# A token-shift evacuation shared out between ScalarE and VectorE, and transposes moved one block back

## The chip, the cores and the metric

The kernel runs on one core of a Trainium2 chip. A core has TensorE (matrix products, PE in the profile; its weight loads are PEld), VectorE (DVE), ScalarE (ACT), GpSimd (POOL) and SyncE (SP), which here issues every DMA. Matrix products land in PSUM, eight banks that TensorE writes and that VectorE and ScalarE read; everything else lies in SBUF or in device memory. The metric is the device time of one execution in microseconds, lower is better; 0.5% of it is 7.8 us.

## The reference

One encoder layer is applied to two token sequences (512 and 256 tokens, width 1024): a hybrid mixer (eight heads of an RWKV-7 recurrence in both directions beside four heads of chunked gated linear attention, GLA), cross-attention to a memory of 256 tokens, and a feed-forward layer, each between RMS norms. What the change touches is the projection into the mixer and the centred shift behind it:

```python
def centred_shift(p, mu_prev, mu_next):
    prev = jnp.pad(p[:, :-1], ((0, 0), (1, 0), (0, 0)))
    nxt = jnp.pad(p[:, 1:], ((0, 0), (0, 1), (0, 0)))
    return p + mu_prev * (prev - p) + mu_next * (nxt - p)

def hybrid_mixer(h, p):
    proj = h @ p['w_in']
    rw = centred_shift(proj[..., :R_COLS], p['mu_prev'], p['mu_next']).astype(jnp.float32)
    gl = proj[..., R_COLS:].astype(jnp.float32)
    mixed = jnp.concatenate([rwkv7_group(rw, p), gla_group(gl, p)], axis=-1).astype(h.dtype)
    return mixed @ p['w_out']
```

The first 1952 columns of the projection (receptance, key, value of the RWKV heads and the small low-rank inputs) are shifted: each token's value is mixed with those of the token before and after it, with weights per column. The other columns (query, key, value, gate of the GLA heads) are not.

## The kernel before

**Tiling.** Activations are held with channels on the 128 partitions and tokens along the free axis. A projection block is 128 columns of `w_in` for all 768 tokens. Products are done in split precision: each operand is a rounded part and a remainder (hi, lo), and one product is three matmuls per 128 input channels (`mm3`, L243 to L250). `load_block` (L214) loads the weights in four pieces through SP, ScalarE rounds them (whi, L149) and VectorE takes the remainder (wlo, L150). `channels_product` (L252) then runs 24 matmuls for the 512-token sequence and 24 for the 256-token one, each sequence into one of the two PSUM buffers with tag "d" (`psd`, L72; the names pd, gvt and others share these two).

**Evacuation.** For a GLA block (`gla_dense`, L475) ScalarE copies the PSUM buffer into an SBUF tile (L482). For an RWKV block (`rkv_block`, L443) `shift_evac` (L318) applies the shift: ScalarE writes (1 − mu_prev − mu_next) times the product (L322), VectorE adds mu_prev times the product moved by one token (L324) and then mu_next times the product moved the other way (L327), both reading PSUM. There are 12 such RWKV blocks (four pairs of heads, `p`, times `i` = 0, 1, 2 for key, receptance, value). The four "small" blocks of the low-rank inputs use the same helper from `small_part` (L360).

**Where the result goes.** The output of a block is a tile `ot` of 128 x 768 with tag "gd". The pool `gdp` has two of these. A store writes it to device memory (`rkvd`, `gqk`, `ggd`). For values (`i` = 2 in `rkv_early`, L448; `g` = 3 in `gla_dense`) it is first turned with tokens on the partitions: `tokens_first` (L464) does six 128 x 128 transposes on TensorE into two "d" buffers (gvt, L470), VectorE copies them into another "gd" tile (L472), and stores follow, four of them for an RWKV pair (`vtd`, L457), one for a GLA block (`gvd`, L486). This second "gd" tile is taken through `gd2` (L459) from the pool in `more[0]`: `gdp` at first, and after GLA head 0 has been traced a pool `gdq` with two buffers of its own (L953).

**Order.** The program is written as a sequence; a scheduler at compile time keeps each engine's queue in the order of its own timeline, by priority (program order, with `tc.high_priority` raising what stands under it), and each engine then executes its queue in order. DMAs are issued in order by SP. The blocks of the stretch are traced in this order: pair 0 (key, receptance, value; L556 to L559), GLA blocks (0, 0), (1, 0), (3, 0), (2, 0) (L819; the first number 0 is the query, 1 the key, 3 the values, 2 the gate), preparation of pair 0 (`begin`), its triangular inverses (`invert`, 62 dependent VectorE operations, L749 to L754), `joined`; `gla_head(0)`; the blocks of pair 1 and (3, 1), (2, 1) (L954), `begin(1)`, `invert(1)`, `gla_head(1)`; (0, 1), (1, 1), (3, 2), (2, 2), `joined(1)`; pair 2 (L960), `gla_head(2)`, (3, 3), (2, 3), `begin(2)`, `invert(2)`, `gla_head(3)`; then the memory's planes (`memory`, L1120, in space that the GLA arena leaves), pair 3 (L1181), and the recurrence itself.

**What a GLA head reads.** `gla_head` (L835) loads its query, key, decay and values into an arena. The values come from `gvd` (L844); the first use of them is the product gds (L900), from which a recurrence of small VectorE operations (L911), the output products (go, L923 and L925), the gate and the store `mixd<-arena` (L949) follow. `begin` loads `wa<-lora` (L646), the decays of the pair, before VectorE's scans and products (L649 to L674).

Of the kernel before, what the change touches and what calls it, by code (L numbers as in the profile page):

```python
# [10 lines left out]
AF = mybir.ActivationFunctionType  # L11
ALU = mybir.AluOpType
# [4 lines left out]
P = 128  # L17
# [15 lines left out]
def kernel(ctx: ExitStack, tc: tile.TileContext, I, y_prompt, y_sample):  # L33
    nc = tc.nc
    act = nc.scalar
    dve = nc.vector
# [3 lines left out]
    def dma(out, in_):  # L40
        return nc.sync.dma_start(out=out, in_=in_)  # L41
# [30 lines left out]
    def psd(name):  # L72
        return ps.tile([P, 512], F32, tag="d", bufs=2, name=name)

    def psm(name):
        return ps.tile([P, 512], F32, tag="m", bufs=2, name=name)
# [15 lines left out]
    hT_hi = hp.tile([P, KD, T], F32R, tag="hh", name="hT_hi")  # L92
    hT_lo = hp.tile([P, KD, T], F32R, tag="hl", name="hT_lo")
# [41 lines left out]
    HS = (slice(0, 64), slice(64, 128))  # L135
# [107 lines left out]
    def mm3(out, pairs):  # L243

        n = 3 * len(pairs)
        i = 0
        for (ah, al), (bh, bl) in pairs:
            for a, b in ((ah, bh), (ah, bl), (al, bh)):
                pe.matmul(out=out, lhsT=a, rhs=b, start=(i == 0), stop=(i == n - 1))  # L249
                i += 1  # L250

    def channels_product(w, m, hi, lo, seqs=SEQS, wc0=0):  # L252

        res = []
        for c0, n in seqs:
            pd = psd("pd")
            mm3(pd[0:m, 0:n], [((wh[:, wc0:wc0 + m], wl[:, wc0:wc0 + m]),
                                (hi[:, k, c0:c0 + n], lo[:, k, c0:c0 + n])) for k, (wh, wl) in enumerate(w)])
            res.append((c0, n, pd))
        return res  # L260
# [4 lines left out]
    def w_cols(c0, n):  # L265
        return w_in[:, c0:c0 + n]
# [48 lines left out]
    def cvc(name, i=0):  # L315
        return cv[:, col[name] + i:col[name] + i + 1]

    def shift_evac(res, mu, dst, m=P):  # L318

        for c0, n, pd in res:  # L320
          with tc.high_priority():
            act.activation(out=dst(c0, n), in_=pd[0:m, 0:n], func=AF.Copy, scale=mu0[0:m, mu:mu + 1])  # L322
            o = dst(c0 + 1, n - 1)
            dve.scalar_tensor_tensor(out=o, in0=pd[0:m, 0:n - 1], scalar=cvc("mu_prev", mu)[0:m, :],  # L324
                                     in1=o, op0=ALU.mult, op1=ALU.add)
            o = dst(c0, n - 1)
            dve.scalar_tensor_tensor(out=o, in0=pd[0:m, 1:n], scalar=cvc("mu_next", mu)[0:m, :],  # L327
                                     in1=o, op0=ALU.mult, op1=ALU.add)

    with tc.high_priority(offset=9000):  # L330
        g_row = lp.tile([1, D], F32, tag="mnxn", bufs=2, name="g_row")
# [19 lines left out]
    for c in (0, 512):  # L351
        t = psm("g_ps")
# [7 lines left out]
    def small_part(i, part):  # L360
# [6 lines left out]
        if part != 1:  # L367
# [7 lines left out]
                      in1=cv[:, col["mu_next"]:col["mu_next"] + 16], op=ALU.add)  # L375
# [14 lines left out]
    for v in ("w0_f", "w0_b", "a0_f", "a0_b", "k_k", "k_a", "lnx_w", "lnx_b"):  # L390
# [11 lines left out]
                      op0=ALU.mult, op1=ALU.add)  # L402
# [10 lines left out]
    gvd = dp.tile([T, 512], F32, name="gvd")  # L413
# [13 lines left out]
    vtd = [dp.tile([2, 64, 6, 128], F32, name=f"vtd{p}") for p in range(4)]  # L427
# [15 lines left out]
    def rkv_block(p, i, dst):  # L443
        c0, mu = ((512, 4), (0, 0), (1024, 8))[i]
        w = load_block([(w_cols(c0 + p * P, P), 0)], P)
        shift_evac(channels_product(w, P, hT_hi, hT_lo), mu + p, dst)

    def rkv_early(p, i):  # L448

        ot = gdp.tile([P, T], F32, tag="gd", bufs=2, name="gd")  # L450
        rkv_block(p, i, lambda c, n: ot[:, c:c + n])
        dma(rkvd[p, i], ot)
        if i == 2:
            vt = tokens_first(ot)
            for h, hs in enumerate(HS):
                for par, ps_ in enumerate(HS):
                    dma(vtd[p][h][:, :, par * 64:par * 64 + 64], vt[ps_, :, hs])  # L457

    def gd2(name):  # L459
        return more[0].tile([P, T], F32, tag="gd", bufs=2, name=name)  # L460

    more = [gdp]

    def tokens_first(ot):  # L464

        vt = gd2("gd")
        for c, n in SEQS:
            pt = psd("gvt")
            for j in range(0, n, P):
                pe.transpose(out=pt[:, j:j + P], in_=ot[:, c + j:c + j + P], identity=ident)  # L470
            with tc.high_priority():
                dve.tensor_copy(out=vt[:, c:c + n], in_=pt[:, 0:n])  # L472
        return vt.rearrange("p (j e) -> p j e", e=P)

    def gla_dense(g, i):  # L475

        c0 = (1952, 2208, 2992, 2464)[g] + i * P
        w = load_block([(w_cols(c0, P), 0)], P)
        ot = gdp.tile([P, T], F32, tag="gd", bufs=2, name="gd")
        for c, n, pd in channels_product(w, P, hT_hi, hT_lo):  # L480
            with tc.high_priority():
                act.activation(out=ot[:, c:c + n], in_=pd[:, 0:n], func=AF.Copy)  # L482
        if g < 3:
            dma((gqk[i % 2], gqk[2 + i % 2], ggd[i])[g], ot)
            return
        dma(gvd.rearrange("(j p) e -> p j e", p=P)[:, :, i * P:(i + 1) * P], tokens_first(ot))  # L486

    if True:
        def stacked(name, groups, shape, put):
# [106 lines left out]
        for i in range(4):  # L596
# [3 lines left out]
            for k0 in range(0, KD, 4):  # L600
# [3 lines left out]
                ot = lp.tile([P, 4, P], F32, tag="mt", bufs=4, name="mt")  # L604
# [11 lines left out]
    for d in range(2):  # L616
        t = mp.tile([P, NCH, 64], F32, tag=f"tt{d}", name=f"tt{d}")
# [195 lines left out]

    def blocks(bs):
        for g, i in bs:
            gla_dense(g, i) if g < 4 else rkv_early(g - 3, i)

    sts = []
    blocks([(0, 0), (1, 0), (3, 0), (2, 0)])  # L819
# [163 lines left out]
    def lay_places():  # L983
        plh, pll = (hp.tile([P, KD * T], F32, tag=n, name="pl_" + n) for n in ("hh", "hl"))
        for t, gs in ((plh, (0, 4)), (pll, (1, 5))):
            for i, g in enumerate(gs):
                whole_place(g, t[:, 2560 * i:2560 * i + 2560])
        place(3, plh[:, 5120:5632], pll[:, 5120:5888], mq1.tile([P, 512], F32, tag="pl3", name="pl3"), plh[:, 5632:6144],
              pll[:, 5888:6144])
        whole_place(2, mq1.tile([P, 2560], F32, tag="pl2", name="pl2"))  # L990
# [188 lines left out]
    mq2 = mq2_cm.__enter__()  # L1179
    mem = memory()  # L1180
    blocks([(6, i) for i in range(3)])  # L1181
    lay_places()
    yas += [gdp.tile([P, T], F32, tag="gd", bufs=2, name=f"ya{i}") for i in range(2)]
    prods(0, (0, 4, 1, 5))
# [20 lines left out]
    for _ in range(BKBUFS):  # L1205
        t = mp.tile([P, 2, T], F32R, tag="bk", bufs=BKBUFS, name="mix_bk")
# [19 lines left out]
    for n in ("snf", "sqf"):  # L1226
        t = mp.tile([P, 2, 512], F32R, tag=n, name="w_" + n)
# [3 lines left out]
    t = mq1.tile([P, 5, 512], F32R, tag="pl2", name="w_pl2")  # L1231
# [82 lines left out]
    with tc.tile_pool(name="op1", bufs=1, reuse_waits="tile") as op1:  # L1314
# [8 lines left out]
        hT_hi, hT_lo = out_projection(op1, wt, mix, x_rows, rows, g_post, x1d, g_pre)  # L1323
# [9 lines left out]
    with tc.tile_pool(name="ao", bufs=1, reuse_waits="tile") as ao:  # L1333
# [18 lines left out]
        for h in range(4):  # L1352
# [16 lines left out]
            for s_, (c0, n) in enumerate(SEQS):  # L1369
# [25 lines left out]
                for e in range(2):  # L1395
# [3 lines left out]
                                     for m in range(2)])  # L1399
                    act.activation(out=oh[:, 2 * h + e, c0:c0 + n], in_=pm[:, 0:n], func=AF.Copy)  # L1400
                    dve.tensor_tensor(out=ol[:, 2 * h + e, c0:c0 + n], in0=pm[:, 0:n], in1=oh[:, 2 * h + e, c0:c0 + n],
                                      op=ALU.subtract)
# [6 lines left out]
        with tc.tile_pool(name="op2", bufs=1, reuse_waits="tile") as op2:  # L1409
# [10 lines left out]
            for i in range(6):  # L1420
                ts_ = slice(i * P, (i + 1) * P)
                pd = (psd, psy)[i % 2]("po")
# [63 lines left out]
    with tc.tile_pool(name="f1", bufs=1, reuse_waits="tile") as f1, tc.tile_pool(name="fw", bufs=1, reuse_waits="tile") as fw:  # L1486
# [98 lines left out]
        h = {"11": blk[0][0], "21": blk[1][0], "22": blk[1][1], "t1": blk[0][1]}  # L1585
# [32 lines left out]
        for at, (f, n) in enumerate(jobs):  # L1618
# [5 lines left out]
            for ct in range(2):  # L1624
# [4 lines left out]
                pd = st["z" if n in (0, 2, 4) else "x", ct][:, 0:384]  # L1629
# [43 lines left out]
        with tc.tile_pool(name="us", bufs=1, side="right", reuse_waits="tile") as us:  # L1673
# [46 lines left out]
            for at, (c, n, s_) in enumerate(jobs):  # L1720
# [3 lines left out]
                for t in range(3):  # L1724
# [4 lines left out]
                    pd = banks["z" if n in (0, 2, 4) else "x", t]  # L1729
# [3 lines left out]
                    if s_ % 2:  # L1733
                        i, half, new = TO[n]
                        i += t
                        o = acc[i][:, CS[half]]
# [34 lines left out]
```

## Time and profile before

| | |
|---|---|
| median of 3 runs | 1554.85 us (1549.77 to 1558.52) |
| the profiled execution | 1548.75 us |
| its span | 1546.6 us |
| mean granted TensorE clock in it | 0.93 |
| instructions | 27578 |
| TensorE matmul, weight load, VectorE, ScalarE, GpSimd busy | 91%, 77%, 70%, 46%, 14% |

The profile shows one execution. A group of instructions is written as its line, engine, operation and the tiles out<-in; "mean ns" is the duration of one of the group. A wait names the instruction that waited and what released it. The chain of work that ended last is followed back from the last instruction of the execution: each piece is what released the next. In the windows, each pair of columns is an engine's busy time and its instructions in that stretch; the last three columns are the granted TensorE clock (1 is full), the share of the DMA engines and their GB/s. All times of single instructions count from the start of the span.

### The profile page before, as it was taken

What the parts mean: (1) busy time and instruction counts of PE and PEld (TensorE: products, weight loads), DVE (VectorE), ACT (ScalarE), POOL (GpSimd) and SP (SyncE); (2) the same over time, 40 slices, a digit from 0 to 9 for tenths busy, and PEclk for the clock granted to TensorE, in tenths of its full rate; (3) what the DMA queues carried; (4) which work ended last, traced back from release to release, by engine and by line L of the source; (5) the groups of instructions that cost most, each with busy time, mean ns of one, the idle gap of its engine ahead of it and who ended that gap; (6) DMA issues with size and microseconds to landing.
All of it is one profiled execution on the core that took longest, in us unless ns stands there. A gap on an engine that the chain in (4) does not pass through costs nothing.

```text
span 1546.6 us, 27578 instructions
## 1 busy us (share of the span) xinstructions
PE 1408.3 (91%) x10238; PEld 1183.6 (77%) x10238; DVE 1076.7 (70%) x1913; ACT 706.0 (46%) x1477; POOL 220.9 (14%) x304
## 2 busy tenths in 40 slices
PE   7998899897799987999699999978999999999996
PEld 6886778775676766777478887868999998787785
DVE  5555896698567994866665554279766667788886
ACT  5664345443423442344353454345554555454342
POOL 5301000000000000003211233320000002132132
PEclk9999899987779996799799999988999999999998
DMA  6687666584468667464452332244554547555334
GB/s 165 177 314 210 171 197 156 167 228 102 128 187 232 180 184 168 106 166 144 128 179 98 107 100 79 82 154 155 196 170 153 181 157 291 155 175 172 120 103 136
DMA packets 279562, 250.30 MB, mean 162 GB/s; under 512 B 89264, under 2 KB 227059, under 8 KB 279428
## 3 DMA queue, kind: packets, MB, share of 16 engines
q1 hardware_dynamic: 279428, 248.54, 53.8%
q8 instruction: 81, 1.33, 0.4%
q14 instruction: 53, 0.43, 0.1%
HBM read 164.11 MB, written 82.58 MB: 160 GB/s over the span
## 4 chain that ended last, share of the span: by engine, by line
PE 59%; DVE 13%; DMA 11%; issue 8%; SPq 3%; ACT 3%; POOL 2%; DVEq 0%; ACTq 0%; POOLq 0%
PE pd L249 19%; PE fx L1548 7%; PE gx L1548 6%; PE fz L1548 5%; PE gz L1548 5%; SPq L41 3%; PE po L249 3%; DMA wraw<-in_w_in_dram 1%; DVE ws L1488 1%; PE hsum L639 1%; DVE wl L1539 1%; DMA raw<-in_w_out_dram 1%; PE xo L249 1%; POOL rs L1264 1%; PE bktp L1028 1%
## 5 line engine op out<-in xcount | busy, mean ns | idle before, releaser
L249 PE MATMUL pd<-hT_hi,whi 128*128 128x256 f32 (+1 forms) x512 | 183.5, 358 | 9.1 <-DVE gd L327 4.1
L249 PE MATMUL pd<-hT_lo,whi 128*128 128x256 f32 (+1 forms) x512 | 180.2, 352 | 0.3 <-DVE hT_lo L208 0.3
L249 PE MATMUL pd<-hT_hi,wlo 128*128 128x256 f32 (+1 forms) x512 | 178.5, 350 | 0.0
L149 ACT ACTIVATE whi<-wraw 128x256 fp32r<-128x256 f32 x192 | 77.5, 415 | 97.2 <-PE pd L249 59.4
L249 PEld LDWEIGHTS pd<-hT_hi,whi 128*128 128x128 f32 x512 | 100.9, 197 | 24.0 <-DVE gd L327 4.0
L150 DVE TENSOR_TENSOR wlo<-wraw,whi 128x256 fp32r<-128x256 f32 x192 | 80.2, 437 | 48.2 <-ACT whi L149 46.6
L249 PEld LDWEIGHTS pd<-hT_lo,whi 128*128 128x128 f32 x512 | 101.0, 197 | 13.1 <-DVE hT_lo L208 0.5
L249 PEld LDWEIGHTS pd<-hT_hi,wlo 128*128 128x128 f32 x512 | 100.2, 196 | 13.2 <-issue 0.5
L150 DVE TENSOR_TENSOR ul<-ur,uh 128x768 fp32r<-128x768 f32 x56 | 75.3, 1351 | 30.2 <-ACT uh L149 17.7
L149 ACT ACTIVATE uh<-ur 128x768 fp32r<-128x768 f32 x56 | 47.2, 845 | 106.6 <-PE gz L1548 51.8
L1538 ACT ACTIVATE wh<-w 128x1024 fp32r<-128x1024 f32 x64 | 67.1, 1053 | 36.7 <-PE fz L1548 24.2
L1539 DVE TENSOR_TENSOR wl<-w,wh 128x1024 fp32r<-128x1024 f32 x56 | 68.2, 1217 | 15.3 <-ACT wh L1538 14.7
L1548 PE MATMUL gx<-wh,uh 128*128 128x512 f32 x192 | 74.9, 397 | 4.2 <-DVE acc L1741 4.2
L1548 PE MATMUL gx<-wl,uh 128*128 128x512 f32 x192 | 75.9, 395 | 0.0
L1548 PE MATMUL gx<-wh,ul 128*128 128x512 f32 x192 | 75.4, 395 | 0.0
L1539 POOL TENSOR_TENSOR wl<-w,wh 128x1024 fp32r<-128x1024 f32 x8 | 20.9, 2610 | 329.3 <-ACT wh L1538 329.3
L1548 PE MATMUL fz<-hh,wh 128*128 128x384 f32 x192 | 66.1, 344 | 1.7 <-ACT wh L1538 1.7
L1548 PE MATMUL fz<-hl,wh 128*128 128x384 f32 x192 | 65.9, 343 | 0.0
L1548 PE MATMUL fz<-hh,wl 128*128 128x384 f32 x192 | 65.2, 344 | 0.6 <-DVE wl L1539 0.6
L1538 ACT ACTIVATE wh<-ws 128x1024 fp32r<-128x1024 f32 x48 | 50.5, 1052 | 27.2 <-PE fx L1548 22.5
L1548 PE MATMUL gz<-wl,uh 128*128 128x512 f32 x144 | 56.9, 395 | 0.0
L249 PE MATMUL pd<-mem_hi,wlo 128*128 128x512 f32 x128 | 56.0, 439 | 0.9 <-DVE wlo L150 0.9
(537 smaller groups left out, 3980.4 us busy)
## 6 DMA issues: line engine op xcount, KB each, us to landing
w<-in_w_ff_dram SPq DMA_DIRECT2D x64, 512.0 KB
ur<-ud SPq DMA_DIRECT2D x56, 384.0 KB
wraw<-in_w_in_dram SPq DMA_DIRECT2D x108, 128.0 KB
ud<-u SPq DMA_DIRECT2D x32, 384.0 KB
ud<-us SPq DMA_DIRECT2D x24, 384.0 KB
wraw<-in_wkv_x_dram SPq DMA_DIRECT2D x64, 128.0 KB
lora<-lo_t SPq DMA_DIRECT2D x20, 384.0 KB
bkg<-bkd SPq DMA_DIRECT2D x24, 256.0 KB
```

The lines of the kernel that those rows point to most:

```text
L41: return nc.sync.dma_start(out=out, in_=in_)
L149: act.activation(out=hi, in_=src, func=AF.Copy)
L150: (lo_eng or pool).tensor_tensor(out=lo, in0=src, in1=hi, op=ALU.subtract)
L249: pe.matmul(out=out, lhsT=a, rhs=b, start=(i == 0), stop=(i == n - 1))
L639: pe.matmul(out=pt[:, 0:n], lhsT=ones_bd, rhs=src[:, c0:c0 + n], start=True, stop=True)
L1028: pe.transpose(out=pt[:, u, :], in_=fl(b_[HS[h], u]), identity=ident[HS[h], HS[h]])
L1264: pool.tensor_tensor(out=rs, in0=ms, in1=neg_half, op=ALU.pow)
L1488: dve.tensor_tensor(out=out, in0=a, in1=b, op=ALU.subtract)
L1538: act.activation(out=hi, in_=t[name], func=AF.Copy)
L1539: lo_eng.tensor_tensor(out=lo, in0=t[name], in1=hi, op=ALU.subtract)
L1548: pe.matmul(out=out, lhsT=a, rhs=b, start=first and i == 0, stop=last and i == n - 1, skip_group_check=True)
```

## The change

`shift_evac` gets a parameter `nx` that gives a scratch tile. Where it is given (the 12 RWKV blocks), ScalarE reads the PSUM buffer a second time and writes mu_next times the moved product into that tile, and VectorE adds the tile to the output, both now in SBUF. The scratch is a "gd" tile from `gd2`, one for each sequence of a block. The small blocks keep the former way. The transposes and stores of values are no longer traced directly behind their block: they are put on a list, `late`, and `blocks` runs what stood on the list before a block after that block has been traced. After the last pair's blocks the list is emptied at once.

```diff
-    def shift_evac(res, mu, dst, m=P):
+    def shift_evac(res, mu, dst, m=P, nx=None):
...
             o = dst(c0, n - 1)
-            dve.scalar_tensor_tensor(out=o, in0=pd[0:m, 1:n], scalar=cvc("mu_next", mu)[0:m, :],
-                                     in1=o, op0=ALU.mult, op1=ALU.add)
+            if nx is None:
+                dve.scalar_tensor_tensor(out=o, in0=pd[0:m, 1:n], scalar=cvc("mu_next", mu)[0:m, :],
+                                         in1=o, op0=ALU.mult, op1=ALU.add)
+            else:
+                t = nx(n - 1)
+                act.activation(out=t, in_=pd[0:m, 1:n], func=AF.Copy, scale=cvc("mu_next", mu)[0:m, :])
+                dve.tensor_tensor(out=o, in0=o, in1=t, op=ALU.add)
...
-        shift_evac(channels_product(w, P, hT_hi, hT_lo), mu + p, dst)
+        shift_evac(channels_product(w, P, hT_hi, hT_lo), mu + p, dst,
+                   nx=lambda n: gd2("nx")[:, 0:n])
...
         if i == 2:
-            vt = tokens_first(ot)
-            for h, hs in enumerate(HS):
-                for par, ps_ in enumerate(HS):
-                    dma(vtd[p][h][:, :, par * 64:par * 64 + 64], vt[ps_, :, hs])
+            def values():
+                vt = tokens_first(ot)
+                for h, hs in enumerate(HS):
+                    for par, ps_ in enumerate(HS):
+                        dma(vtd[p][h][:, :, par * 64:par * 64 + 64], vt[ps_, :, hs])
+            late.append(values)
...
-        dma(gvd.rearrange("(j p) e -> p j e", p=P)[:, :, i * P:(i + 1) * P], tokens_first(ot))
+        late.append(lambda: dma(gvd.rearrange("(j p) e -> p j e", p=P)[:, :, i * P:(i + 1) * P], tokens_first(ot)))
...
     def blocks(bs):
         for g, i in bs:
+            fs = late[:]
+            late.clear()
             gla_dense(g, i) if g < 4 else rkv_early(g - 3, i)
+            for f in fs:
+                f()
...
     blocks([(6, i) for i in range(3)])
+    for f in late:
+        f()
```

More of the change, by code (lines that the diff above doesn't have):

```diff
@@ L462 @@
     more = [gdp]
+    late = []
     def tokens_first(ot):
```

## The prediction

> **What bounds the kernel now.** I read the page first, then the windows around the stretch that the change touches (60 to 450 us from the span's start; the blocks with a centred shift and the value blocks all lie there), then TensorE's waits, then the chain that ended last.
>
> ```profile
> PE 1408.3 (91%) x10238; PEld 1183.6 (77%) x10238; DVE 1076.7 (70%) x1913; ACT 706.0 (46%) x1477; POOL 220.9 (14%) x304
> PE 59%; DVE 13%; DMA 11%; issue 8%; SPq 3%; ACT 3%; POOL 2%; DVEq 0%; ACTq 0%; POOLq 0%
> 246.00:288.00 42.00, 38.40 (x420) 30.91 (x419) 19.98 (x35) 20.33 (x53) 2.42 (x7) 0.96 0.74 195
> 288.00:334.00 46.00, 43.72 (x333) 35.29 (x333) 42.67 (x69) 23.89 (x66) 1.04 (x4) 0.96 0.60 175
> 334.00:382.00 48.00, 37.45 (x229) 27.71 (x229) 45.43 (x112) 14.80 (x39) 3.15 (x8) 0.79 0.52 144
> 382.00:402.00 20.00, 6.96 (x150) 5.49 (x150) 7.89 (x19) 11.54 (x35) 0.00 (x0) 0.50 0.60 128
> ```
>
> TensorE is 91% busy over the span, so the average says "TensorE". The four windows (PE, PEld, DVE, ACT, POOL busy, then granted clock, DMA) say otherwise for this stretch: from 288 to 382 VectorE is busy 88.1 of 94 us, and from 382 to 402 nothing is busy, with PE at 7 of 20 us: a chain of latencies. Its links stand in the chain of work that ended last, with VectorE's two evacuations of the last gated-linear-attention (GLA) head between them:
>
> ```profile
> 386.99 1.14 DVE L947 SCALAR_TENSOR_TENSOR arena<-got,cv,arena 128x512 f32<-128x512 f32 x2
> 392.92 2.75 DMA mixd<-arena
> 395.77 3.79 ACT mem_hi L149 x12
> 402.10 6.24 PE pd L249 x22
> ```
>
> Head 3 is done on VectorE at 388.13, its store is issued 4.8 us later, the memory's planes take its arena when that has landed, and only then the next projection block runs. Whatever TensorE wins before 362 counts only if this store comes earlier. Where TensorE waits for the work that the change edits:
>
> ```profile
> PE gvt L470 <- ACT gd L482: 6.1, 2, 5.9
> PE gvt L470 <- DVE gd L327: 5.5, 3, 2.9
> PE pd L249 <- DVE gd L327: 4.1, 4, 2.0
> PE pd L249 <- DVE gd L472: 1.2, 1, 1.2
> 145.08 0.69 PE L470 MATMUL gvt<-ident,gd 128*128 128x128 f32 x2 [5.90 <-ACT gd L482]
> 187.72 0.58 PE L249 MATMUL pd<-hT_hi,whi 128*128 128x256 f32 x1 [2.02 <-DVE gd L327]
> 212.46 0.66 PE L470 MATMUL gvt<-ident,gd 128*128 128x128 f32 x2 [2.89 <-DVE gd L327]
> 307.60 0.79 PE L249 MATMUL pd<-hT_hi,whi 128*128 128x512 f32 x1 [1.66 <-DVE gd L327]
> ```
>
> The waits sum to 6.1 + 5.5 + 4.1 + 1.2 = 16.9 us. 11.6 are transposes (gvt) that stand in PE's queue ahead of the next block's matmuls and wait for the block's evacuation; 4.1 are matmuls that wait for a PSUM buffer until the second VectorE addition (L327) has read it.
>
> **The change part by part.** *Durations.* 12 blocks with two sequences each, 24 evacuations:
>
> ```profile
> L322 ACT ACTIVATE gd<-pd,mu 128x512 f32<-128x512 f32 x11 | 7.6, 688 | 28.9 <-PE pd L249 20.9 <-issue 8.0
> L322 ACT ACTIVATE gd<-pd,mu 128x256 f32<-128x256 f32 x11 | 5.1, 465 | 0.0
> L327 DVE SCALAR_TENSOR_TENSOR gd<-pd,cv,gd 128x511 f32<-128x511 f32 x11 | 8.2, 745 | 0.1
> L327 DVE SCALAR_TENSOR_TENSOR gd<-pd,cv,gd 128x255 f32<-128x255 f32 x11 | 5.2, 474 | 0.1
> L150 DVE TENSOR_TENSOR mem_lo<-raw,mem_hi 128x256 fp32r<-128x256 f32 x16 | 5.6, 417 | 8.8 <-ACT mem_hi L149 8.8
> L708 DVE TENSOR_TENSOR kk<-kk,wa 128x768 f32<-128x768 f32 x4 | 3.8, 956 | 4.7 <-ACT wa L707 4.7
> ```
>
> ScalarE gains 12 x (0.688 + 0.465) = 13.8 us: the new read of 511 or 255 columns is the same form as L322. On VectorE a sum of two SBUF tiles takes 417 ns at 256 and 956 ns at 768 columns, so by a straight line about 685 ns at 511: against 745 and 474 each pair saves 0.06 + 0.06, and 12 pairs 1.4 us. VectorE is therefore hardly relieved; what changes is when the PSUM buffer comes free. Before, it is free after L322, L324 and L327; L327 stands in VectorE's queue behind other work. Now the last reader is on ScalarE, which is 52% busy from 288 to 334 where VectorE is 93%. I take the 4.1 us of waits on L327 as gone; the bounds are 0 (ScalarE's read waits as long) and 4.1.
>
> *What the waits cost beside themselves.* After them the granted clock is low (the column after PE busy):
>
> ```profile
> 213.00:221.00 8.00, 8.00 (x26) 0.67 0.45 100
> 147.00:152.00 5.00, 5.00 (x24) 0.69 0.48 131
> 340.00:348.00 8.00, 8.00 (x27) 0.71 0.86 218
> ```
>
> That is 8 x 0.33 + 5 x 0.31 + 8 x 0.29 = 6.5 us of TensorE. [...] I go by the trace: with the waits, 16.9 + 6.5 = 23.4 us of TensorE are at stake.
>
> *What the move of the values costs.* Their transposes, copies and DMAs come after the next block's matmuls. For the GLA values this delays what the head needs. Head 3:
>
> ```profile
> 354.35 0.37 SPq L41 DMA_DIRECT2D gvd<-gd  x1
> 357.12 0.37 SPq L41 DMA_DIRECT2D arena<-gvd  x1
> 362.32 1.71 PE L900 MATMUL gds<-arena 64*128 64x128 f32 x16
> 226.99 8.45 PE pd L249 x48
> 268.93 3.94 DMA gqk<-gd
> 281.24 2.98 DMA gvd<-gd
> 284.69 4.02 DMA wa<-lora
> ```
>
> The first three are from the timelines of the SP queue and of TensorE, the others from the chain. A block (48 matmuls) takes 8.45 us, so gvd and arena<-gvd move back by that, less what TensorE is earlier. Today gds waits for its turn behind the block, not for the values; a block later it waits for them. In the SP queue arena<-gvd stands still until gvd has landed, and what is queued behind it waits too, as today: at 284.69 that is wa<-lora, the start of the next pair's decays on VectorE. Each pair's four vtd stores move back in that queue likewise; nothing near needs them.
>
> *Buffers.* The new tile nx takes from the same two "gd" buffers as the block's output, and from the second pair only after head 0 is traced. So the first pair's values (until the next block's transposes) and the block after them hold both; the copy of the transposes waits until that block's output has been stored, about 0.36 (L482, 256 columns, estimate from the nearest form, L322 at 0.465, at most that) + 3.94 (the store gqk<-gd, issue to landing) plus the hand-overs, some 5 us, in which the transposes hold both PSUM buffers, the next matmuls wait behind them in PE's queue, and the copy may hold up what stands behind it in VectorE's (the head's products and the weights' remainders, wlo). This happens twice (after the first pair's values and after GLA value block 0): 0 to 10 us of new PE waits. I take 8.7 us, near the full cost, because at these places no other matmuls are left to fill in; it eats the 5.9 + 1.2 + 1.6 us which the early stretch wins (145 to 152).
>
> *Sum.* Early stretch: 8.7 won, 8.7 lost: 0. From 187 to 348: 23.4 − 8.7 = 14.7 us of TensorE won, then 8.45 given back at head 3 because its values come a block later: 6.2 us. The other path to the store, VectorE's 88 of 94 us, can start earlier only as wa<-lora does; TensorE leads there by 2.02 + about 3.9 of the 5.5 + 2.6 of clock, 8.5 us, so this path allows 6.2. About 1 us I leave to the added ScalarE work: its 13.8 us are covered by idle time (ScalarE is busy 59 of the 136 us from 246 to 382), and if that cover is gone it costs up to 13.8. **Forecast: 5 us less** than this execution.
>
> **The rivals.** *(a) The waits come through in full.* If the new order hides the values' lateness (another head's work in between) and VectorE's path starts earlier with TensorE, 14.7 us come through, and up to 20 if the early stretch keeps 5 of its 8.7: 15 us faster. For it: from 246 to 288 VectorE is idle for 22 of 42 us, so its path has room to move. Against it: 93% and 95% busy VectorE after that.
>
> *(b) Slower: ScalarE stands still behind the second read.* The new read may run only after L324 has read the same PSUM buffer; if so, it waits at the head of ScalarE's queue for VectorE. L324 is often late:
>
> ```profile
> 318.82 0.45 ACT L322 ACTIVATE gd<-pd,mu 128x256 f32<-128x256 f32 x1
> 326.32 0.47 DVE L324 SCALAR_TENSOR_TENSOR gd<-pd,cv,gd 128x255 f32<-128x255 f32 x1
> 299.60 0.69 ACT L322 ACTIVATE gd<-pd,mu 128x512 f32<-128x512 f32 x1 [2.75 <-PE pd L249]
> 303.52 0.75 DVE L324 SCALAR_TENSOR_TENSOR gd<-pd,cv,gd 128x511 f32<-128x511 f32 x1
> ```
>
> That is 7.05 and 3.23 us in which ScalarE, which also rounds the weights (whi) that TensorE needs, would do nothing, 10.3 for these two of 24 (the second after 0.69 of its own read); before, VectorE held up only itself. It decides once more than the 5 us of the forecast reach TensorE; if the other 22 bring half as much again and all of it does, it is 15 − 5: 10 us slower. [...]
>
> *(c) It does not do what it says:* the last pair's values (6,2) are flushed at once, and the order on every engine is made anew, so waits may only change their names: 0 us.
>
> **How the numbers follow.** The forecast (with c, both within 0.5%, which is 7.8 us and about what a measurement of this kernel can tell from no change) gets 0.42, (a) 0.34, (b) 0.24. This execution took 1548.75 us, of which 1546.6 are span; the median of the runs shown is 1554.85, so I carry the difference: 1554.85 − 5 = 1549.9, say 1550. (a) is 1540, (b) 1565. The range takes in both with their bounds: 20 us won gives 1535, 10 lost 1565, and some two more: 1534 to 1567. Chances: faster 0.34, same 0.42, slower 0.24.
>
> **What would show it.** Right: gvt no longer waits for L327 or L482; pd no longer waits for L327; 213 to 221 at a clock near 1; gds of head 3 waits for arena<-gvd; mixd<-arena about 5 us earlier. Wrong: gvt or its copy waits for a store of gd in the first pair (the buffers cost more); idle time of ScalarE ended by VectorE's L324 with whi late behind it (b); or PE's waits in 187 to 348 gone and 392.92 hardly moved, which would put VectorE's path ahead of everything.

## The result, and the profile after

The changed kernel takes 1571.5 us (median of 13 runs) against 1554.85 us for the kernel before, run on the same chip. The ratio is 1.0084, with a 95% interval of 1.0057 to 1.0111: slower by 0.84%, some 13 us, and by at least 9. The forecast was 5 us less, 1550, in a range of 1534 to 1567; the change went the other way, and the median lies outside the range. The ratio is formed without two of the 13 runs of the changed kernel, 1621.67 and 7264.55 us, which were slow ones and raise its median by about 2 us. The profiled execution of the changed kernel took 1567.51 us, with a span of 1565.8.

Its page begins like the one before: TensorE's work is unchanged, VectorE's sum is unchanged, and ScalarE has 24 instructions and 8.5 us more.

```profile
PE 1406.2 (90%) x10238; PEld 1182.8 (76%) x10238; DVE 1076.7 (69%) x1913; ACT 714.5 (46%) x1501; POOL 223.3 (14%) x304
```

VectorE's second addition costs what the rows of before foretold. This is the view of line 333, where it now reads SBUF (duration as shortest, median and longest in ns; the short ones are those of 255 columns):

```profile
L333 DVE TENSOR_TENSOR gd<-gd,nx x22: 408/550/695, 89.4 to 450.2; 128x511 f32<-128x511 f32 x11, 128x255 f32<-128x255 f32 x11
```

So the loss isn't in the price of an instruction. TensorE's waits between 100 and 420 us of the span (who waited, for whom: us in total, times, longest):

```profile
PE gs L886 <- DVE arena L877: 10.7, 1, 10.7
PE go L937 <- DVE arena L925: 7.8, 2, 7.5
...
PE pd L249 <- ACT nx L332: 5.0, 4, 2.9
...
PE gds L914 <- DMA arena<-gvd: 1.3, 1, 1.3
...
PE gvt L480 <- ACT gd L492: 0.6, 2, 0.4
```

The transposes (gvt), which waited 11.6 us before, wait 0.6. The low clock behind those waits is gone too, as these windows show (length, then busy time and instructions of PE, PEld, DVE, ACT and POOL, then the granted clock, the DMA share and GB/s); 147 to 152 and 213 to 221 were granted 0.69 and 0.67 before. The first line is the kernel before, the others are the changed kernel:

```profile
140.00:147.00 7.00, 0.71 (x3) 0.32 (x3) 6.66 (x8) 3.03 (x6) 3.01 (x3) 0.73 0.79 207
140.00:147.00 7.00, 5.20 (x26) 4.41 (x27) 6.07 (x8) 3.81 (x7) 1.41 (x5) 1.00 0.68 166
147.00:152.00 5.00, 4.50 (x62) 3.81 (x60) 4.94 (x7) 2.36 (x6) 0.39 (x3) 1.00 0.24 71
213.00:221.00 8.00, 8.00 (x51) 7.12 (x50) 6.92 (x17) 5.19 (x14) 0.00 (x0) 1.00 0.53 113
```

TensorE did win what it was to win: it has the last projection block ahead of GLA head 3, with the transposes of the head's values, behind it at 353.7, where it ended this work at 362.4 before. It then has nothing to do. The head's first products (gs), which ran ahead of the end of that block before (the last at 353.0), come only at 364.39 in TensorE's timeline of the changed kernel, and the one behind the recurrence at 381.77:

```profile
353.35 0.38 PE L480 MATMUL gvt<-ident,gd 128*128 128x128 f32 x2
364.39 1.68 PE L886 MATMUL gs<-arena 64*64 64x64 f32 x48 [10.66 <-DVE arena L877]
...
368.57 3.07 PE L914 MATMUL gds<-arena 64*128 64x128 f32 x16 [1.04 <-ACT arena L900]
...
381.77 0.70 PE L937 MATMUL go<-arena 128*64 128x128 f32 x4 [7.53 <-DVE arena L925]
```

Those products wait for VectorE, which turns to head 3 when head 2's output is done. All four heads use one arena, so they follow one another, and head 0 is the first that its values reach late. Here are the SP queue and TensorE of the kernel before (the store of head 0's values, their load into the arena, the product that reads them, the store of the head's output):

```profile
149.13 0.42 SPq L41 DMA_DIRECT2D gvd<-gd  x1
152.11 0.37 SPq L41 DMA_DIRECT2D arena<-gvd  x1
164.59 1.71 PE L900 MATMUL gds<-arena 64*128 64x128 f32 x16 
207.82 0.32 SPq L41 DMA_DIRECT2D mixd<-arena  x1
```

and the same four steps in the changed kernel:

```profile
161.64 0.42 SPq L41 DMA_DIRECT2D gvd<-gd  x1
165.32 2.78 SPq L41 DMA_DIRECT2D arena<-gvd  x1
173.47 1.71 PE L914 MATMUL gds<-arena 64*128 64x128 f32 x16 [1.35 <-DMA arena<-gvd]
219.89 0.34 SPq L41 DMA_DIRECT2D mixd<-arena  x1
```

The values are stored 12.5 us later, loaded 13.2 us later, read 8.9 us later, and the head's output is stored 12.1 us later. The wait that TensorE itself shows is only 1.35 us, since the order made anew has put other work ahead of the product: the lateness is not in a wait on TensorE, it is in when the head ends. The values of the other heads are not late in this way: their loads (arena<-gvd) are issued 3.0 us earlier, 0.9 later and 3.5 later than before (226.91, 285.15, 360.63). The outputs of the four heads (the end of their last VectorE operation) are at 207.8, 261.1, 336.4 and 388.1 before and at 219.9, 271.8, 355.2 and 395.5 after: later by 12.1, 10.7, 18.8 and 7.4 us.

VectorE meanwhile stands still where it was to get ahead. Between 255 and 270 it is busy 1.81 us, against 9.13 before (from 240 to 270 together, 14.38 against 17.62). The first line is before, the second after:

```profile
255.00:270.00 15.00, 15.00 (x188) 12.58 (x188) 9.13 (x12) 9.19 (x21) 0.00 (x0) 1.00 0.72 200
255.00:270.00 15.00, 14.08 (x159) 10.61 (x159) 1.81 (x3) 9.28 (x33) 0.00 (x0) 0.89 0.62 150
```

The keys of the pair are normalised later (kk, line 708 before, line 718 after), the load wa<-lora is issued behind that, and VectorE's last stretch begins later. VectorE before, then VectorE, SP and ScalarE after:

```profile
281.26 0.96 DVE L708 TENSOR_TENSOR kk<-kk,wa 128x768 f32<-128x768 f32 x1
288.73 1.76 DVE L649 TENSOR_TENSOR_SCAN wb<-scan_mask,wa 128x768 f32<-128x768 bf16 x1 [6.52 <-DMA wa<-lora]
```

```profile
289.05 0.94 DVE L718 TENSOR_TENSOR kk<-kk,wa 128x768 f32<-128x768 f32 x1
290.02 0.34 SPq L41 DMA_DIRECT2D wa<-lora  x1
294.30 1.76 DVE L659 TENSOR_TENSOR_SCAN wb<-scan_mask,wa 128x768 f32<-128x768 bf16 x1 [3.98 <-DMA wa<-lora]
394.38 1.14 DVE L961 SCALAR_TENSOR_TENSOR arena<-got,cv,arena 128x512 f32<-128x512 f32 x2
400.34 0.35 SPq L41 DMA_DIRECT2D mixd<-arena  x1
402.94 0.42 ACT L149 ACTIVATE mem_hi<-raw 128x256 fp32r<-128x256 f32 x1 [2.24 <-DMA mixd<-arena]
```

The load is issued at 290.02 instead of 284.69, the scan starts 5.6 us later, the store of head 3 is issued at 400.34 instead of 392.92, and the memory's planes begin 7.2 us later. From there the same instructions come mostly some 4 to 9 us later than in the trace of before until about 550, and near 20 us later towards the end. The chain that ended last on this page holds only the last few stores (its shares are all 0%), so it says nothing here.

### The profile page after: what moved, and what is told of

Its sections match the earlier page's. It is cut to its first block, busy times and chain, and to the rows that moved or that the text cites. A ratio compares the mean times of both kernels' runs of the same rounds, so it can differ in the third digit from the quotient of the medians.

```text
span 1565.8 us, 27574 instructions
## 1 busy us (share of the span) xinstructions
PE 1406.2 (90%) x10238; PEld 1182.8 (76%) x10238; DVE 1076.7 (69%) x1913; ACT 714.5 (46%) x1501; POOL 223.3 (14%) x304
## 5 line engine op out<-in xcount | busy, mean ns | idle before, releaser
L249 PE MATMUL pd<-hT_hi,whi 128*128 128x512 f32 (+1 forms) x512 | 179.9, 351 | 8.8 <-ACT nx L332 5.0
L249 PE MATMUL pd<-hT_lo,whi 128*128 128x512 f32 (+1 forms) x512 | 176.8, 346 | 0.3 <-DVE hT_lo L208 0.3
L1564 PE MATMUL gz<-wh,uh 128*128 128x512 f32 x144 | 56.1, 396 | 0.7 <-ACT uh L149 0.7
```

What stands on the lines that cost most here:

```text
L1564: pe.matmul(out=out, lhsT=a, rhs=b, start=first and i == 0, stop=last and i == n - 1, skip_group_check=True)
```

## The experiments

Each kernel was timed in five rounds against the kernel before on the same chip. Four theories stand in the expectations. **A**: the values, a block later, hold up VectorE's path to head 3's store. **B**: ScalarE stands behind its second read, waiting for VectorE's first addition. **C**: the order of every engine, made anew by the compile-time scheduler, costs the time, not the edits themselves. **D**, added later: the four heads follow one another through the arena, and the lateness of each head's values is handed on until it sets when VectorE's last stretch starts.

| kernel | order of the engines | ratio to before, 95% |
|---|---|---|
| the change | made anew | 1.0084 (1.0057 to 1.0111) |
| e1_shift_only | made anew | 1.0055 (1.0029 to 1.008) |
| e2_late_only | made anew | 1.022 (1.0179 to 1.0261) |
| e3_gla_at_once | made anew | 1.0159 (1.0122 to 1.0196) |
| e4_rkv_at_once | made anew | 1.0132 (1.0093 to 1.0172) |
| p1_shift_old_order | held, before's | 0.9995 (0.9963 to 1.0027) |
| p2_late_old_order | held, before's | 1.0174 (1.012 to 1.0228) |
| p3_both_old_order | held, before's | 1.0205 (1.0157 to 1.0253) |
| t1_old_order_behind_402 | held: the change's, before's behind 402 us | 1.0075 (1.0037 to 1.0112) |
| p4_rkv_late_old_order | held, before's | 1.0062 (1.0029 to 1.0095) |
| p5_gla_late_old_order | held, before's | 1.015 (1.0122 to 1.0179) |
| p6_shift_rkv_late_old_order | held, before's | 1.0109 (1.0065 to 1.0154) |
| q1_new_order_old_shift | held, the change's | 1.022 (1.0191 to 1.025) |
| x1_values_block_earlier | made anew | 1.0035 (1.001 to 1.0059) |
| x2_before_block_earlier | made anew | 1.0188 (1.0151 to 1.0225) |
| x3_earlier_rkv_at_once | made anew | 1.0136 (1.0101 to 1.0171) |

**First: the parts of the change, one at a time.** The shift alone, with values at once (pair 0's values, which are traced outside `blocks`, still come one block later):

```diff
-            fs = late[:]
-            late.clear()
             gla_dense(g, i) if g < 4 else rkv_early(g - 3, i)
-            for f in fs:
-                f()
+            while late:
+                late.pop(0)()
```

> The second read of PSUM goes to ScalarE and VectorE adds from SBUF, as in the change, but the values are transposed right after their own block, as before. Theory A (the values' lateness holds up the VectorE path of the next pair: wa<-lora leaves SP's queue 5.3 us later, 290.02 for 284.69, and the end of the last head's store 7.6 us later): without the lateness this kernel is at the time before or up to 5 us below it (1550 to 1555). Theory B (ScalarE waits behind its second read for VectorE and the weights come late): all the loss is here, 8 to 13 us above the time before. Theory C (the order of all instructions is made anew, and the loss behind 555 us is an accident of that): anything from -10 to +15 us, and the shifts against before behind 555 us differ from those of the change.

The late values alone:

```diff
-        shift_evac(channels_product(w, P, hT_hi, hT_lo), mu + p, dst,
-                   nx=lambda n: gd2("nx")[:, 0:n])
+        shift_evac(channels_product(w, P, hT_hi, hT_lo), mu + p, dst)
```

> The values are transposed one block later, as in the change, but both additions are VectorE's from PSUM, as before. Theory A: the loss of the change, 8 to 13 us above the time before, with wa<-lora of the second pair issued near 290 us and mixd<-arena of the last head near 400 us. Theory B: at the time before or up to 5 us below it. Theory C: -10 to +15 us, in no relation to the other run.

The whole change with the GLA heads' values at once, and with the RWKV pairs' values at once:

```diff
-        late.append(lambda: dma(gvd.rearrange("(j p) e -> p j e", p=P)[:, :, i * P:(i + 1) * P], tokens_first(ot)))
+        dma(gvd.rearrange("(j p) e -> p j e", p=P)[:, :, i * P:(i + 1) * P], tokens_first(ot))
```

> The change, but the gated-linear-attention values are transposed right after their own block; only the RWKV values come a block later. Theory A in its narrow form (the gvd store that stands ahead of wa<-lora in SP's queue is what is late): near the time before, 0 to 4 us above. Theory B: the loss of the change, 8 to 13 us above the time before. Theory C: -10 to +15 us.

```diff
-            late.append(values)
+            values()
```

> The change, but the RWKV values are transposed right after their own block; only the gated-linear-attention values come a block later. Theory A in its narrow form: the loss of the change, 8 to 13 us above the time before. Theory B: the same loss. Theory C: -10 to +15 us.

Measured: +8.5 us for the shift alone, +34 for the late values alone, +25 and +21 where one of the two groups of values goes back, all of them slower than the kernel before; e2 and e3 are also clearly slower than the whole change (e4's interval overlaps that of the change). The parts don't add up: where the GLA values go back to their place, the time rises by some 12 us over that of the whole change, which no theory of late values explains. Each of these edits has also made the scheduler write another order. So C is at least a disturbance of every such trial, and the parts can't be told apart in this way.

**Second: the same edits with the order held.** Every engine's queue is tied to a written order, by a dependency without a semaphore from each instruction to the one ahead of it. The order is that of the kernel before (an added instruction stands where its data allow it), or of the changed one:

```diff
+def pin_order(tc, nc):
...
+    for seq in json.loads(zlib.decompress(base64.b85decode(ORDER))):
+        at, prev = 0, None
+        for step in seq:
+            at += step
+            if prev is not None:
+                tc.add_manual_dep(traced[at], traced[prev].name, info, reason="order")
+            prev = at
```

p1 has the second read in 18 of the 24 evacuations (pairs 1 to 3, with a scratch tile of its own for pairs 1 and 2) and the values at once. p2 has all values a block later, as in the change (the last pair's are not), and no second read. p3 has both.

> Each engine is held to the order in which it issued in the kernel before; in the shifts of pairs 1 to 3 (18 of 24) the second read is on ScalarE, put where VectorE's L324 ended before, and the sum from SBUF stands at the place of L327; the values stay where they were; the product lands in a tile of its own for pairs 1 and 2. Theory B (ScalarE behind its second read makes the weights late): 3 to 10 us above the time before. Theory C (the change's parts cost little, the order made anew is what costs): within -4 to +2 us, since the 4.1 us of matmuls that wait for L327 go at best and ScalarE has room.

> Each engine held to the order before, but the transposes of the values, their copies, their stores and the load of the last head's values from them stand behind the next block's matmuls (pair 0 to 2 and all four heads; the last pair as before). Theory A (lateness of the values): the last head's state products (L900) move back by about 8.5 us, mixd<-arena of the last head comes 6 to 8 us later, and the whole is 5 to 9 us above the time before. Theory C: within -6 to +3 us, since 11.6 us of waiting transposes go and the late loads are covered.

> The two together in the order before: the whole change but for pair 0's second reads, with nothing else moved. If the change itself is what costs (theories A or B): 8 to 13 us above the time before, as measured for the change. If the order made anew costs (theory C): the sum of the two runs before it, within -8 to +5 us.

t1 is the whole change with its own order ahead of 402 us, and before's order behind.

> The whole change; what the kernel before starts ahead of 402 us stands in the order that the change made, everything behind that in the order before (with pair 3's second reads where L324 ended). Theory C for the second loss: the shift of 7 us at 400 us stays and nothing is added behind it, so 5 to 8 us above the time before. Theories A and B: the loss behind 555 us is the change's own, so 11 to 17 us above, as the change.

With the order held, the second read is worth nothing (0.9995) and the lateness costs 27 us (1.0174). With both the interval (1.0157 to 1.0253) overlaps that of the lateness alone. t1 is as slow as the change: a new order behind 402 us isn't needed for the loss, and what is ahead of 402 is enough for it. p3 holds the change's edits but for pair 0's second reads; it is 32 us slower than the kernel before, where the change in its own order is 13 slower, and these intervals are far apart. So for these edits before's order is the worse one by some 19 us: the new order hides part of what the lateness costs. TensorE's waits between 100 and 420 say what happens. In p1:

```profile
PE gvt L480 <- DVE gd L333: 7.6, 3, 3.6
PE gvt L480 <- ACT gd L492: 6.7, 2, 5.9
...
PE pd L249 <- ACT nx L332: 2.0, 1, 2.0
```

The waits for a PSUM buffer behind the second read fall from 4.1 us to 2.0, as the edit means them to, and those of the transposes rise from 11.6 to 14.3: nothing is left over. In p2:

```profile
PE gds L913 <- DMA arena<-gvd: 22.1, 4, 8.6
...
PE pd L249 <- DVE gd L481: 7.2, 4, 3.7
...
PE gvt L479 <- ACT gd L491: 2.2, 6, 0.8
```

The transposes' waits fall from 11.6 to 2.2, and the heads' first product now waits 22.1 us for its values: 2.3, 8.2, 3.0 and 8.6 at heads 0 to 3. The next block's matmuls wait another 7.2 for PSUM buffers until the late transposes are copied out of them (line 481; 1.2 before). This wait takes the place of the one removed, and here it shows on TensorE, because nothing can be put in front of it.

**Third: which values, and what the second read does in the change's order.** p4 and p5 hold before's order with only the RWKV pairs' or only the GLA heads' values late; p6 is p4 with the second read; q1 holds the change's order on every engine, with late values, but with VectorE reading PSUM twice again.

> The order before, both additions on VectorE; only the RWKV values of pairs 0 to 2 are transposed a block later, the values of the four GLA heads right after their own block. Theory D (the four heads follow one another through one arena, each needs its values before its state products, and this chain, not TensorE's blocks, sets the end; so only the heads' values can cost): 0.98 to 1.002 of the time before, -6 to +3 us, since the waits of gvt for L327 at 208.9, 212.5 and 337.4 (5.5 us) go. Theory A in its wide form (lateness of any values costs through SP's queue and the buffers): half of what both cost, +10 to +15 us.

> The order before, both additions on VectorE; only the GLA heads' values are transposed a block later. Theory D: nearly all of what both cost, +20 to +30 us, with the state products (gds) waiting for arena<-gvd in all four heads, some 22 us in sum. Theory A in its wide form: +10 to +15 us.

> The order before with the second read on ScalarE in pairs 1 to 3 and the RWKV values a block later, the heads' values at once: the change without what theory D holds to be its cost. Theory D: -8 to +3 us of the time before. If the change itself costs in another way (B): +3 to +10 us.

> Every engine in the order that the whole change made, but the second addition is VectorE's from PSUM again and ScalarE's 24 second reads are left away. Theory B (the waits of 5.0 us of matmuls and 6.8 us of weight loads for nx in the changed kernel's page are the loss): 5 to 10 us below the change, that is 1.000 to 1.005 of the time before. Theory D (the loss is the heads' chain): within 3 us of the change, 1.006 to 1.011 of the time before.

The GLA values make most of it, 23 us (p5), and it is the same wait as in p2. The RWKV values, which no head waits for, still cost 10 us in this order (p4): a block later their transposes meet those of the GLA values, and the second set waits for the copy of the first. The lines that show it, of p5 and of p4:

```profile
PE gds L913 <- DMA arena<-gvd: 23.1, 4, 9.8
```

```profile
PE gvt L479 <- DVE gd L481: 8.9, 4, 5.3
```

p6 (+17 us) lies above p4 (+10), but their intervals overlap, so what the second read adds there isn't settled. In q1 the change's order is 34 us slower than before; with the second read it is 13 us slower. There the read is worth some 21 us, and the intervals are far apart. Its line is of the kind that the change was to take away; in the changed kernel the same kind, for nx, is 5.0 us in all:

```profile
PE pd L249 <- DVE gd L328: 20.5, 4, 10.5
```

This ends B as the cause in this order. Its mechanism is there: in the changed kernel ScalarE stands idle ahead of the second read for VectorE's first addition, 7.8 us in 7 places. Two of them as ScalarE's timeline has them, and the sum from the view of line 332:

```profile
183.22 0.69 ACT L332 ACTIVATE nx<-pd,cv 128x511 f32<-128x511 f32 x1 [1.57 <-DVE gd L324]
...
185.72 0.47 ACT L332 ACTIVATE nx<-pd,cv 128x255 f32<-128x255 f32 x1 [1.54 <-DVE gd L324]
```

```profile
  DVE gd L324: 7.8, 7
```

But 24 second reads share those 7.8 us, and without them TensorE waits 15 us longer in the same order.

**Fourth: the remedy that D asks for.** If late values are the trouble, tracing each GLA value block one block earlier should give the time back. x1 does so in the changed kernel, x2 in the kernel before, where no value is late, and x3 is x1 with the RWKV values at once:

```diff
-    blocks([(0, 0), (1, 0), (3, 0), (2, 0)])
+    blocks([(0, 0), (3, 0), (1, 0), (2, 0)])
...
-        blocks([(4, i) for i in range(3)] + [(3, 1), (2, 1)])
+        blocks([(4, 0), (4, 1), (3, 1), (4, 2), (2, 1)])
...
-        blocks([(0, 1), (1, 1), (3, 2), (2, 2)])
+        blocks([(0, 1), (3, 2), (1, 1), (2, 2)])
...
-        blocks([(5, i) for i in range(3)])
+        blocks([(5, 0), (5, 1), (3, 3), (5, 2)])
...
-        blocks([(3, 3), (2, 3)])
+        blocks([(2, 3)])
```

> The whole change, in an order made anew, but each GLA value block (3, i) is traced one block earlier, so that its transposes, now a block late, stand about where they stood before the change. Theory D (the lateness of the heads' values): the loss goes, 0.995 to 1.003 of the time before, and head 0's output ends near 208 us as before (the change: 219.9). Theory C (any order made anew costs): 1.005 to 1.02, as the other runs with orders of their own.

> The kernel before with the GLA value blocks traced one block earlier and nothing of the change. Theory D: the values are there earlier than the heads can use them, so 0.997 to 1.004 of the time before. Theory C: 1.005 to 1.02.

> The change with the RWKV values at once, and the GLA value blocks one block earlier with their values a block late. Theory D: against the same kernel with the blocks in their places (1.013) it regains 10 to 20 us, 0.995 to 1.006 of the time before. Theory C: 1.005 to 1.02.

x1 is the best of the versions with late values, 5 us behind the kernel before instead of 13. The ends of the heads' outputs on VectorE, and the issue of head 3's store, in six of the traces:

| kernel | head 0 | head 1 | head 2 | store of head 3 |
|---|---|---|---|---|
| before | 207.8 | 261.1 | 336.4 | 392.92 |
| the change | 219.9 | 271.8 | 355.2 | 400.34 |
| e1_shift_only | 208.4 | 270.6 | 357.5 | 398.77 |
| e4_rkv_at_once | 216.1 | 264.2 | 343.3 | 392.67 |
| p1_shift_old_order | 209.8 | 263.3 | 342.3 | 398.67 |
| x1_values_block_earlier | 208.4 | 257.9 | 354.8 | 401.91 |

In x1 heads 0 and 1 are back in their places, as D asks. But head 2 is as late as in the change, and head 3's store comes no earlier, so what x1 regains doesn't stand where D puts it. e1 says the same: all four heads have their values at once, and still head 2's output is 21 us late. So the 18.8 us of head 2 in the change need no late head 0. In before's order the last step of head 2's recurrence on VectorE is at 316.05; in the change and in e1 the recurrence is spread among VectorE's products for the pair (bk) and its second scan, and ends 21 to 22 us later. The three lines are of before, of the change and of e1:

```profile
316.05 0.35 DVE L911 SCALAR_TENSOR_TENSOR arena<-arena,dec 64x128 f32<-64x128 f32 x1
...
337.05 0.72 DVE L925 SCALAR_TENSOR_TENSOR arena<-arena,dec 64x128 f32<-64x128 f32 x2
...
338.26 0.35 DVE L923 SCALAR_TENSOR_TENSOR arena<-arena,dec 64x128 f32<-64x128 f32 x1
```

Nor does head 3's store measure the loss. In p1, whose time equals that of before, the store of the one execution traced is 5.8 us late; in e4, which is 21 us slower than before, it is in its old place, and TensorE stands for 12.26 us at a merge of the triangular inverses instead. The stores of e1, p1, e4 and x1, and that wait in e4:

```profile
398.77 0.35 SPq L41 DMA_DIRECT2D mixd<-arena  x1
398.67 0.35 SPq L41 DMA_DIRECT2D mixd<-arena  x1
392.67 0.33 SPq L41 DMA_DIRECT2D mixd<-arena  x1
401.91 0.60 SPq L41 DMA_DIRECT2D mixd<-arena  x1
...
403.71 0.31 PE L806 MATMUL merge<-tdz,lsb 32*32 32x32 f32 x2 [12.26 <-DMA tdz<-td]
```

x3, which should have been no worse than x1, is at 1.0136; and x2, which has no part of the change in it, is at 1.0188. The kernels with an order made anew lie between 5 us (x1) and 34 us (e2) above the kernel before, so the 8 us that x1 regains can't be claimed for D. No version ran faster than the kernel before; p1 is equal to it.

**The rest of the loss, behind 402 us.** The profiled execution of the change loses another 10 us between 700 and 760. There TensorE stands for 6.83 us behind VectorE, which itself waits 3.21 us for a load (fb<-lora), and the granted clock is 0.50 from 704 to 728:

```profile
708.40 0.69 PE L1060 MATMUL rec<-pl_hh 64*64 64x64 f32 x6 [6.83 <-DVE pl_hh L1037]
```

t1 has before's order in that stretch and the same ratio as the change, so the new order there isn't needed for the loss. How much a single execution can lose at that place, with before's order, p1 shows. Its TensorE timeline, then the first and the fifth of five windows of 4 us, all with a granted clock of 0.50:

```profile
712.82 0.70 PE L1078 MATMUL rec<-pl 128*64 128x64 f32 x8 [3.11 <-ACT pl L1073]
```

```profile
712.00:716.00 4.00, 3.18 (x26) 2.50 (x27) 1.53 (x5) 2.07 (x7) 3.26 (x7) 0.50 0.78 215
...
728.00:732.00 4.00, 4.00 (x43) 2.88 (x42) 0.37 (x2) 0.54 (x2) 0.00 (x0) 0.50 0.59 163
```

In the kernel before the same product waits 0.96 us, and the clock stays at 1.00 in every window from 704 to 740:

```profile
705.64 0.45 PE L1066 MATMUL rec<-pl 128*64 128x64 f32 x8 [0.96 <-ACT pl L1061]
```

p1's profiled execution took 1565.66 us, 8.3 above its median of 1557.34; that of before lies 6.1 below its median, that of the change 4.0 below. So two profiles can differ by 14 us where the medians are equal, and the 7.2 us at 402 and the 20 us at the end of the change's profile are each known to no better than several us. That the loss is 13 us comes from the timed rounds, and that it is there without the new order behind 402 from t1; its split over the stretches of the trace stays open.

## Why the prediction was wrong, step by step

**What bounds the kernel.** Right in its main point: the store of head 3 opens the next projection, and TensorE's lead counts only if this store comes earlier. The last condition of the prediction came true word for word: TensorE's waits were gone, TensorE was 8.7 us ahead at head 3, and the store wasn't earlier; it was 7.4 us later in the trace. "Nothing is busy" from 382 to 402 is too strong: ScalarE is, for 11.54 of the 20 us. And e4 shows that the store isn't the only thing that can hold up the next projection: there it is on time, and the merge of the inverses is late.

**The durations.** Right on VectorE: the addition from SBUF takes 0.408 us at its shortest (255 columns) and 0.695 at its longest (511), where the prediction had 0.417 (read from a row of 256 columns) and 0.685 (worked out). VectorE's sum didn't move, though, where 1.4 us less were worked out. ScalarE's busy time rose by 8.5 us where 13.8 were worked out: the 24 second reads do take 13.8 (8.2 and 5.6), and which of its other work shrank is open.

**The waits that go.** The transposes' 11.6 us went, nearly whole (0.6 is left), and most of their low clock with them: 1.00 from 147 to 152 and from 213 to 221, and 0.88 from 340 to 348, where 0.69, 0.67 and 0.71 were granted before. The 4.1 us for the PSUM buffer did not go, as the step had it: in the change they are 5.0 us on ScalarE's second read. With before's order held, taking L327 off the buffer was worth nothing measurable (p1, 0.9995). Only q1 shows what the 5.0 mean, since in the change's order the former addition costs 20.5. A wait of the order before is no measure of what an operation is worth in the order after.

**The buffers of the first pair.** Wrong: the step charged 8.7 us there, enough to eat the whole early win. From 140 to 147 TensorE is busy for 5.20 us, and was for 0.71, and ScalarE's evacuations behind that begin 5 to 9 us earlier (148.87 for 154.89, 166.78 for 175.26). TensorE's only waits there for the copy of the transposes are 0.5 and 1.8 us, where one of 1.2 stood before.

**The values a block later: the step that failed.** "8.45 given back at head 3" names the right mechanism, and the right size for that head (8.6 in p2), but at one of the four places where it acts, and the last one. The rows of head 0 stood in the same trace (gvd at 149.13, arena<-gvd at 152.11, gds at 164.59), with 12.5 us between load and product that a block and more could use up; the sum doesn't have them. Held in the old order, the lateness of all values costs 27 us, net of the transposes' waits that it removes; 22.1 stand as waits of gds at four heads, where the prediction had 8.45 for one. In the change's order little of this wait is left on TensorE (1.35 us, at head 0), only head 0's values are loaded much later, and the heads' outputs are 7 to 19 us late.

**VectorE's path "allows 6.2".** Wrong in sign. The step let VectorE's last stretch start as much earlier as TensorE leads, in an order that it took as given. In the change that stretch starts 5.6 us later, behind wa<-lora, and that behind kk, which came 7.8 us later while VectorE stood idle. And an early start isn't enough: in e1 kk is at 280.48, ahead of the 281.26 of before, and head 2's output is 21 us late all the same, since the order of VectorE is another. How the 13 us of the change divide between head 0's lateness and the new order isn't shown; e1 (8.5 us slower, with all heads' values at once) says only that the new order can cost much of it by itself.

**The rivals.** (a), all waits come through, is out. (b), the slower one, gave 1565, near the time measured, by luck, for its reason doesn't hold: q1 shows the second read as a gain of some 21 us in the change's order, and p1 as nothing in before's. (c) had the new order as a way to nothing; the runs show it as a term of its own. The second read costs nothing in before's order (p1) and 8.5 us in an order made for it (e1, where pair 0's reads and late values come on top), and the edits that cost 32 us in before's order (p3, without pair 0's second reads) cost 13 in their own. x2, which only moves blocks, is 29 us slower; what of that is the move itself can't be told.

## What to carry to other kernels

When a step is moved back, look for its reader at every place where the step occurs, the first one ahead of all, and follow the chain that hands its lateness on; a wait that vanishes from the busy engine's list may have become a later end somewhere else. To tell the parts of a change from the order that a scheduler makes of them, hold the order: free reorderings of this kernel differ by more than the change itself is worth. But what is measured with the order held is the price in that order; in its own, the same change cost less than half. An engine that leads the path by 8.7 us has won nothing if the chain beside it isn't moved.

## What the runs showed of the hardware

A wait of 3.11 us on TensorE was followed by 20 us at a granted clock of 0.50 (712 to 732 in p1), though TensorE was busy for 19.2 of them. Half the clock for 20 us costs some 10 us by estimate from these numbers, three times the wait. The next windows were granted 0.54 (732 to 736) and 1.00 (736 to 740).

ScalarE and VectorE did not read the same PSUM buffer at once: at all 24 evacuations of the changed kernel the second read began after the first addition had ended, between 0.03 and 2.4 us behind it, and in 7 places ScalarE stood idle for it, 7.8 us in all. Whether the two could read one buffer at once, no run here shows.

Executions of one program differ by more than the range that three runs had shown for the kernel before: its 13 runs lie between 1549.67 and 1565.16 us.
